# An RWKV-7 block: receptances read from their PSUM banks, key scaling on VectorE, the state summed in the bank, and the second inversion issued inside the recursion

## The chip, the cores and the metric

The kernel runs on one core of a Trainium2 chip. The metric is the device time of one execution in microseconds (us). The engines are named as in the profile: PE is TensorE's matmul, PEld its weight load, DVE is VectorE, ACT is ScalarE, POOL is GpSimd, SP is the queue that issues the DMAs. PSUM is the memory with eight banks that PE writes its products to; a bank holds 512 float32 values in each of 128 partitions.

## The reference

The program is a trunk of two layers on 512 positions of width 1024: SwiGLU, an attention mixer, SwiGLU; then SwiGLU, RWKV-7 time mixing, SwiGLU. Only the time mixing of the second layer changes:

```python
xr, xw, xk, xv, xa, xg = [h + xx * mix[i] for i in range(6)]   # xx: the row before, minus h
r, k, v = xr @ w_r, xk @ w_k, xv @ w_v
decay = exp(-exp(-softplus(-(w0 + tanh(xw @ w1) @ w2)) - 0.5))
a = sigmoid(a0 + (xa @ a1) @ a2)
kk = heads(k * k_k);  kk = kk / norm(kk)
k = k * (1.0 + (a - 1.0) * k_a)
# 16 heads of 64, one state S (64 x 64) a head, over the 512 positions:
S_t = S_{t-1} (diag(w_t) - kk_t^T (kk_t * a_t)) + v_t k_t^T;   y_t = S_t r_t
y = group_norm(y) + (sum(r * k * r_k) per head) * v
out = (y * g) @ w_o
```

r is called the receptance. The sequence is worked through in eight chunks of 64 positions: inside a chunk the recursion becomes a triangular system, whose inverse is applied, and only the state goes from chunk to chunk.

## The kernel before

Data lie features by positions: a tile of 128 features (two heads of 64) has 512 positions. There are two head groups, `sg` 0 and 1, of four such tiles (eight heads) each. A projection (`project(half, ...)`) makes four tiles at once, in four PSUM banks of the tag "rm" (there are four in all): for each of eight input blocks k it multiplies the mixed input with the weights into all four banks, in three passes of float32 split in two parts (L286 to L288 in `mm3`), 96 matmuls a half. The input blocks are mixed by `mixed(i, c)`: ACT scales (L1079), DVE adds the shifted row (L1081), ACT rounds to the high part (L1090), and DVE or POOL takes the residual (L1092). For the receptance (i = 0) the mixes are made anew for each half, in two alternating buffers.

The order in the program is: keys k half 0, prep of group 0, k half 1, v half 0 and 1, inversion of group 0, prep of group 1, receptance r half 0, `rw_prep2(0)`, r half 1, `rw_prep2(1)`, inversion of group 1, recursion of group 0, recursion of group 1. A scheduler then sets each engine's order from the dependencies, its own costs and the edges `self.after(a, b)`, which keep a behind b in the order without a wait on the chip. Each engine works through its own queue in that order.

`rw_prep` makes, for one tile, the decays, the normalised and scaled keys and the operands of the recursion: two matmul groups of "lora" products (`rq` banks), L1052 spreads the keys' norms, L1245 to L1261 are wide operations of 128 x 512 on DVE, L1248 is the key's product with its factor on POOL, L1268 multiplies operands chunk by chunk on PE, L1269 masks the result, and it goes to DRAM (L1282) to be laid out for the inversion. The scaled keys go to DRAM too (L1249).

`rw_inverse` loads that (`lin`), works off 31 pairs of DVE operations (L1321, L1325), reorders on ACT (L1326), writes the factors to DRAM (`tout`), reads them back, and finishes by a back-substitution in four blocks of 32 x 32 matmuls (L1353, L1360) with copies L1355 and L1362.

`rw_prep2` takes the receptances that ACT copied from the banks (L1102), multiplies them on POOL into the planes of the recursion (L1293), and on DVE with the reloaded keys (L1292, L1294) for the sum over each head on PE (L1297), copied by L1299.

`rw_recur(sg)` runs the chunks c = 0 to 7. A step solves for the chunk (L1422, L1427, ACT's L1433, L1437), copies the solution to `sv` (ACT L1440), forms the state's increment (L1445), multiplies the old state with its decay on POOL (L1448) and adds both on DVE (L1449; L1451 copies at c = 0). Then `rw_ties` prepares the next chunk (matmuls L1385, masks on DVE L1388, transposes L1391), and L1456 and L1461 make the outputs, which ACT copies (L1464).

Of the kernel before, what the change touches and what calls it, by code (L numbers as in the profile page):

```python
# [11 lines left out]
F32 = mybir.dt.float32  # L12
F32R = mybir.dt.float32r
AF = mybir.ActivationFunctionType
ALU = mybir.AluOpType
# [4 lines left out]
P = 128  # L20
D = 1024
S = 512
NCH = D // P
# [22 lines left out]
class Trunk:  # L46
# [1008 lines left out]
    def rwkv(self, gain):  # L1055
        nc, mm = self.nc, self.nc.tensor.matmul
# [8 lines left out]
        h = self.x  # L1065
# [6 lines left out]
        self.first = self.mid = None  # L1072
        n_mix = [0]

        def mixed(i, c):

            n = n_mix[0] = n_mix[0] + 1
            t = self.row("mx", 3) if i == 2 else self.rows[:, n % 2, :]
            ins = nc.scalar.activation(t, h[c], AF.Copy, scale=v["mix1"][:, i, c : c + 1])  # L1079
            self.after(ins, (self.mid, None, None, self.first)[i])  # L1080
            nc.vector.scalar_tensor_tensor(  # L1081
                out=t[:, 1:], in0=h[c][:, : S - 1], scalar=v["mix"][:, i, c : c + 1], in1=t[:, 1:],
                op0=ALU.mult, op1=ALU.add,
            )
# [5 lines left out]
            nc.scalar.copy(m[:, 0, :], t)  # L1090
# [4 lines left out]
        r_t, k_t = [None] * NCH, [None] * NCH  # L1095

        def evac_feature(dst):
            def f(half, ps):
                all4 = self.t("kr", [4, S], 2)
                for i in range(4):  # L1100
                    t = dst[4 * half + i] = all4[:, i, :]
                    nc.scalar.copy(t, ps[i])  # L1102
            return f

        vd = self.dram.tile([4, P, D], F32, name="vd")
        vcd = self.dram.tile([4, P, D], F32, name="vcd")
        kd = self.dram.tile([NCH, P, S], F32, name="kd")

        def evac_v(half, ps):

# [14 lines left out]

        def project(half, xm, evac, natural, i_mix=None):

            w, xs = [], xm if xm is not None else {}
            ps = [self.bank("rm", 4) for _ in range(4)]

            def tile(k, b):
                first, last = k == 0, k == NCH - 1
                if natural:
                    self.mm3(ps[b], tuple(t[:, b * P : (b + 1) * P] for t in xs[k]), w[k], first, last)
                else:
                    self.mm3(ps[b], tuple(t[:, b * P : (b + 1) * P] for t in w[k]), xs[k], first, last)

            for k in range(NCH):
                if k % 2 == 0:
                    w += self.next_w()  # L1140
                if half == 0 or xm is None:
                    if i_mix == 2:
                        normed(k)
                    xs[k] = mixed(i_mix, k)
                if k < 6:
                    for b in range(4):
                        tile(k, b)
                if k == 0 and half == 1 and not natural:
                    self.first = self.last_mm
# [9 lines left out]
        xm, evac = {}, evac_feature(k_t)  # L1159
        self.rwkv_hids()  # L1160
        project(0, xm, evac, False, 2)
        self.lora_hidden(lora_out, rstd)
        self.rr = {}
        self.rw = dict(r=r_t, k=k_t, vd=vd, vcd=vcd, kd=kd, w2a2=self.next_w())
        self.rw_norm(0)
        self.rw_prep_all(0)
        project(1, xm, evac, False)
        self.rw_norm(1)
        xm = {}
        project(0, xm, evac_v, True, 3)  # L1170
# [2 lines left out]
        self.rw_inverse(0, mid)  # L1173
        self.rw_prep_all(1)

        evac = evac_feature(r_t)
# [34 lines left out]
    def rw_prep(self, m):  # L1211

        nc, mm = self.nc, self.nc.tensor.matmul
# [31 lines left out]
        nc.vector.scalar_tensor_tensor(out=kk, in0=k, scalar=col("kk2"), in1=ps, op0=ALU.mult, op1=ALU.mult)  # L1245
        kx = cum
        nc.scalar.activation(kx, a, AF.Identity, scale=col("ka"), bias=col("ka1"))
        nc.gpsimd.tensor_tensor(out=k, in0=kx, in1=k, op=ALU.mult)  # L1248
        nc.sync.dma_start(rw["kd"][m], k)  # L1249
        nc.vector.scalar_tensor_tensor(out=a, in0=a, scalar=1.0, in1=kk, op0=ALU.add, op1=ALU.mult)  # L1250
        nc.vector.scalar_tensor_tensor(
            out=ar[:, 0, :, 1:], in0=ar[:, 0, :, 1:], scalar=-2.0, in1=ar[:, 1, :, : C - 1], op0=ALU.mult, op1=ALU.mult
# [29 lines left out]
                nc.sync.dma_start(dst, u[p0 : p0 + 32, :, 32 * s : 32 * s + 32])  # L1282
        yield

    def rw_prep2(self, sg):

        nc, rw = self.nc, self.rw
        ps = self.bank("rq", 3)[:8, :]
        for j in range(4):
# [3 lines left out]
            nc.gpsimd.tensor_tensor(out=rp, in0=r, in1=rp, op=ALU.mult)  # L1293
            nc.vector.scalar_tensor_tensor(  # L1294
                out=r, in0=r, scalar=self.v["rk"][:, m : m + 1], in1=k, op0=ALU.mult, op1=ALU.mult
            )
            nc.tensor.matmul(ps, self.sel[:, j, :], r, start=j == 0, stop=j == 3)  # L1297
        y = rw["r"][4 * sg][:8]
        nc.vector.tensor_copy(y, ps)  # L1299
        self.head_keep("b", sg, y)  # L1300

# [62 lines left out]
    def rw_ties(self, sg, c):  # L1364
# [20 lines left out]
                    prev, ins = ins, mm(ps[h][to, j, :], pp["kb"][e][own, c, :], pp["ar"][own, :, c, :], start=True, stop=True)  # L1385
                    self.after(ins, prev)
        for h in range(2):
            nc.vector.tensor_tensor(out=am[:, h], in0=ps[h], in1=mask, op=ALU.mult)  # L1388
# [14 lines left out]
    def rw_recur(self, sg):  # L1403

        nc, mm = self.nc, self.nc.tensor.matmul
        pairs = [self.rw[4 * sg + j] for j in range(4)]
# [9 lines left out]
        for c in range(NC):  # L1416
# [23 lines left out]
                nc.scalar.copy(sv[oth, h], ps[oth])  # L1440
            if c < NC - 1:
                ps = b2[:, 1]
                for j in range(4):
                    for h, (own, _) in enumerate(self.halves):
                        moved = mm(ps[own, j, :], bn[:, j, h, :], sv[:, h, j, :], start=True, stop=True)  # L1445
                if c:
                    pend = self.pend[:, sg, :, c, None].to_broadcast([P, 4, C])
                    nc.gpsimd.tensor_tensor(out=part, in0=st, in1=pend, op=ALU.mult)  # L1448
                    nc.vector.tensor_tensor(out=new, in0=ps, in1=part, op=ALU.add)  # L1449
# [158 lines left out]
```

## Time and profile before

| | us |
| --- | --- |
| median of three runs | 2159.97 |
| lowest, highest | 2156.48, 2165.26 |
| the profiled execution | 2156.56 |
| its span, first to last instruction | 2154.9 |

In the profiled execution PE is busy 2104.1 us, DVE 1165.4, ACT 781.2, POOL 192.7, and the mean granted clock of TensorE is 0.989. The part of the program that the change touches lies between about 1440 and 1735 us. A group of the profile is read: line, engine, operation, output and inputs by the program's names, shape, count, then the busy time with the mean of one in ns, then the idle time of the engine ahead of it and what ended that. A name like `const` or `inv` is that of the memory in which several tiles share a place: `const<-ra,const` at L1388 is the mask of the recursion.

### The profile page before, as it was taken

What the parts mean: (1) busy time and instruction counts of PE and PEld (TensorE: products, weight loads), DVE (VectorE), ACT (ScalarE), POOL (GpSimd) and SP (SyncE); (2) the same over time, 40 slices, a digit from 0 to 9 for tenths busy, and PEclk for the clock granted to TensorE, in tenths of its full rate; (3) what the DMA queues carried; (4) which work ended last, traced back from release to release, by engine and by line L of the source; (5) the groups of instructions that cost most, each with busy time, mean ns of one, the idle gap of its engine ahead of it and who ended that gap; (6) DMA issues with size and microseconds to landing.
All of it is one profiled execution on the core that took longest, in us unless ns stands there. A gap on an engine that the chain in (4) does not pass through costs nothing.

```text
span 2154.9 us, 28881 instructions
## 1 busy us (share of the span) xinstructions
PE 2104.1 (98%) x11623; PEld 1697.2 (79%) x11623; DVE 1165.4 (54%) x1595; ACT 781.2 (36%) x1180; POOL 192.7 (9%) x208
## 2 busy tenths in 40 slices
PE   8999999999999999999999999999978999999999
PEld 6888887767988888888888888777646768888887
DVE  5444444467568645446644454657675555444443
ACT  4222223355316433334433333472434434222222
POOL 2000001010002000002000000222451101000000
PEclk9999999999999999999999999999989999999999
DMA  5232323411117664555555555447743342232332
GB/s 180 78 110 86 109 87 108 125 57 47 28 45 231 217 200 158 183 187 180 181 182 162 183 160 189 170 137 234 220 131 85 102 131 86 83 113 93 98 103 59
DMA packets 264095, 286.59 MB, mean 133 GB/s; under 512 B 45140, under 2 KB 221420, under 8 KB 263961
## 3 DMA queue, kind: packets, MB, share of 16 engines
q1 hardware_dynamic: 261848, 282.65, 42.1%
q10 hardware_dynamic: 2112, 2.10, 0.3%
q8 instruction: 91, 1.49, 0.3%
q14 instruction: 44, 0.35, 0.1%
HBM read 229.85 MB, written 56.68 MB: 133 GB/s over the span
## 4 chain that ended last, share of the span: by engine, by line
PE 91%; DVE 6%; DMA 1%; issue 1%; ACT 1%; POOL 0%; SPq 0%; DVEq 0%; ACTq 0%; POOLq 0%
PE b L286 22%; PE b L288 22%; PE b L287 22%; PE am L286 3%; PE am L287 3%; PE am L288 3%; PE rm L286 1%; PE rm L287 1%; PE rm L288 1%; DVE const L1321 1%; PE wo L286 1%; PE rq L1021 1%; DVE inv L1325 1%; PE wo L287 1%; PE wo L288 1%
## 5 line engine op out<-in xcount | busy, mean ns | idle before, releaser
L287 PE MATMUL b<-xg,parts 128*128 128x512 f32 x1408 | 548.5, 390 | 0.0
L286 PE MATMUL b<-xg,parts 128*128 128x512 f32 x1408 | 547.0, 391 | 1.2 <-ACT xg L385 0.7
L288 PE MATMUL b<-xg,parts 128*128 128x512 f32 x1408 | 547.7, 390 | 0.0
L258 DVE TENSOR_TENSOR parts<-const,parts 128x1024 fp32r<-128x1024 f32 (+2 forms) x320 | 362.3, 1139 | 290.7 <-ACT parts L257 290.3
L257 ACT CAST parts<-const 128x1024 fp32r<-128x1024 f32 (+2 forms) x320 | 312.1, 977 | 469.2 <-PE b L287 391.0
L286 PEld LDWEIGHTS b<-xg,parts 128*128 128x128 f32 x1408 | 264.5, 188 | 57.2 <-ACT xg L385 1.1
L287 PEld LDWEIGHTS b<-xg,parts 128*128 128x128 f32 x1408 | 264.6, 188 | 56.6 <-issue 1.0
L288 PEld LDWEIGHTS b<-xg,parts 128*128 128x128 f32 x1408 | 264.4, 188 | 55.2 <-DVE parts L258 0.3
L288 PE MATMUL b<-act,parts 128*128 128x512 f32 x704 | 273.3, 389 | 0.0
L287 PE MATMUL b<-act,parts 128*128 128x512 f32 x704 | 273.2, 389 | 0.0
L286 PE MATMUL b<-act,parts 128*128 128x512 f32 x704 | 272.4, 390 | 0.0
L373 POOL TENSOR_TENSOR ssum<-ssum,sq 128x512 f32<-128x512 f32 x42 | 65.4, 1557 | 1201.2 <-ACT sq L372 534.4
L287 PEld LDWEIGHTS b<-act,parts 128*128 128x128 f32 x704 | 132.2, 188 | 27.5
L288 PEld LDWEIGHTS b<-act,parts 128*128 128x128 f32 x704 | 132.1, 188 | 27.3
L286 PEld LDWEIGHTS b<-act,parts 128*128 128x128 f32 x704 | 132.1, 188 | 27.2
L498 DVE SCALAR_TENSOR_TENSOR const<-b,const 128x512 f32<-128x512 f32 x128 | 87.3, 687 | 111.3 <-PE b L288 111.3
L291 ACT CAST act<-u 128x512 fp32r<-128x512 f32 x88 | 54.7, 622 | 245.4 <-DVE u L484 245.3
L483 DVE TENSOR_TENSOR u<-b,rstd 128x512 f32<-128x512 f32 x88 | 60.5, 690 | 146.6 <-PE b L288 146.4
L92 ACT ACTIVATE g<-g 128x512 f32<-128x512 f32 x88 | 55.1, 630 | 189.6 <-DVE g L478 189.6
L478 DVE TENSOR_TENSOR g<-b,rstd 128x512 f32<-128x512 f32 x88 | 60.3, 688 | 95.4 <-PE b L288 95.3
L292 DVE TENSOR_TENSOR act<-u,act 128x512 fp32r<-128x512 f32 x88 | 60.6, 689 | 36.8 <-ACT act L291 36.5
L484 DVE TENSOR_TENSOR u<-u,g 128x512 f32<-128x512 f32 x88 | 60.5, 691 | 2.7
(331 smaller groups left out, 2594.3 us busy)
## 6 DMA issues: line engine op xcount, KB each, us to landing
const<-in_ffn_w_gate_dram SPq DMA_DIRECT2D x88, 512.0 KB
const<-in_ffn_w_up_dram SPq DMA_DIRECT2D x88, 512.0 KB
parts<-pparts SPq DMA_DIRECT2D x68, 512.0 KB
parts<-parts SPq DMA_DIRECT2D x68, 512.0 KB
const<-in_ffn_w_down_dram SPq DMA_DIRECT2D x64, 512.0 KB
const<-in_ffn_w_down_dram SPq DMA_DIRECT2D x48, 256.0 KB
const<-in_attn_w_in_dram SPq DMA_DIRECT2D x24, 512.0 KB
lora<-pparts SPq DMA_DIRECT2D x8, 576.0 KB
```

What stands on the lines that cost most here:

```text
L92: ins = nc.scalar.activation(out, in_, func, **kw)
L257: self.nc.scalar.copy(hi[:r, :n], raw[:, :n])
L258: self.lo_engine.tensor_tensor(out=lo[:r, :n], in0=raw[:, :n], in1=hi[:r, :n].bitcast(F32), op=ALU.subtract)
L286: self.after(mm(out, lhs[0], rhs[0], start=start, stop=False), self.gate)
L287: mm(out, lhs[0], rhs[1], start=False, stop=False)
L288: self.last_mm = mm(out, lhs[1], rhs[0], start=False, stop=stop)
L292: self.nc.vector.tensor_tensor(out=lo, in0=t, in1=hi.bitcast(F32), op=ALU.subtract)
L373: nc.gpsimd.tensor_tensor(out=ssum, in0=ssum, in1=sq, op=ALU.add)
L478: nc.vector.tensor_tensor(out=g, in0=ps[i], in1=rstd, op=ALU.mult)
L483: nc.vector.tensor_tensor(out=u, in0=ps[2 + i], in1=rstd, op=ALU.mult)
L484: nc.vector.tensor_tensor(out=u, in0=u, in1=gs[i], op=ALU.mult)
L498: nc.vector.scalar_tensor_tensor(out=self.x[c], in0=ps, scalar=0.5, in1=self.x[c], op0=ALU.mult, op1=ALU.add)
```

## The change

The receptance's four banks are no longer copied by ACT. `rw_prep2` is called at the end of each receptance half and reads the banks with two DVE operations each: the product into the plane (L1282 of the changed kernel) and the product with the keys (L1283). The scaled keys stay in SBUF under a tag of their own; their way over DRAM is gone. The key's product with its factor is on DVE (L1239). The receptance's mixes have three buffers, and all mixes of a half hang on one point in the order. `dep` is the fifth input block's last matmul of the projection before (`self.mid`), and `r` in `rw_prep2` is the bank itself. In the recursion eight matmuls with an identity put the decayed state into the bank ahead of the increment's eight, and ACT copies the sum. The second inversion is issued in the first step of group 0's recursion.

```diff
@@ mixed(), project()
-            self.after(ins, (self.mid, None, None, self.first)[i])
+            self.after(ins, dep)
...
-            if i == 0:
-                m = self.shaped(self.parts_all[:, (n % 2) * 2 * S : (n % 2 + 1) * 2 * S], [2, S])
+            if i == 0 and n % 3:
+                m = self.shaped(self.parts_all[:, (n % 3 - 1) * 2 * S : n % 3 * 2 * S], [2, S])
             else:
-                m = self.pair("xm", 9, F32R)
+                m = self.pair("xm" if i else "xr", 9, F32R)
@@ rwkv()
-        project(0, None, evac, False, 0)
-        self.rw_prep2(0)
-        project(1, None, evac, False, 0)
-        self.rw_prep2(1)
-        self.rw_inverse(1, None)
-        self.rw_recur(0)
+        for half in range(2):
+            project(half, None, self.rw_prep2, False, 0)
+        self.rw_recur(0, lambda: self.rw_inverse(1, self.masked))
@@ rw_prep()
-        nc.gpsimd.tensor_tensor(out=k, in0=kx, in1=k, op=ALU.mult)
-        nc.sync.dma_start(rw["kd"][m], k)
+        nc.vector.tensor_tensor(out=k, in0=kx, in1=k, op=ALU.mult)
@@ rw_prep2(sg, rs)
-            k, r, rp = self.row("kback"), rw["r"][m], self.plane(sg, j, 1)
-            self.after(nc.sync.dma_start(k, rw["kd"][m]), self.mid)
-            nc.gpsimd.tensor_tensor(out=rp, in0=r, in1=rp, op=ALU.mult)
+            t, rp = self.row("rb"), self.plane(sg, j, 1)
+            nc.vector.tensor_tensor(out=rp, in0=r, in1=rp, op=ALU.mult)
             nc.vector.scalar_tensor_tensor(
-                out=r, in0=r, scalar=self.v["rk"][:, m : m + 1], in1=k, op0=ALU.mult, op1=ALU.mult
+                out=t, in0=r, scalar=self.v["rk"][:, m : m + 1], in1=rw["k"][m], op0=ALU.mult, op1=ALU.mult
             )
@@ rw_recur(sg, among=None)
                 if c:
                     nc.gpsimd.tensor_tensor(out=part, in0=st, in1=pend, op=ALU.mult)
-                    nc.vector.tensor_tensor(out=new, in0=ps, in1=part, op=ALU.add)
-                else:
-                    nc.vector.tensor_copy(new, ps)
+                    for j in range(4):
+                        for h, (own, _) in enumerate(self.halves):
+                            ins = mm(ps[own, j, :], self.ident[own, own], part[own, j, :], start=j == 0, stop=False)
...
+                nc.scalar.copy(new, ps)
                 am2, bn2, sv2 = self.rw_ties(sg, c + 1)
+                if c == 0 and among:
+                    among()
```

How this stands in the queues is seen at three places. The first is DVE's order at the end of prep of group 1. Before (`ra` is a bank of the ties, `rm` a bank of the receptance, `kr` its copy):

```order
L1269 TENSOR_TENSOR heads<-rq,const 128x512
L1388 TENSOR_TENSOR const<-ra,const 128x512 x2
L1269 TENSOR_TENSOR heads<-rq,const 128x512
L1294 SCALAR_TENSOR_TENSOR kr<-kr,const,kback 128x512 x2
L1269 TENSOR_TENSOR heads<-rq,const 128x512
L1294 SCALAR_TENSOR_TENSOR kr<-kr,const,kback 128x512 x2
L1299 COPY kr<-rq 8x512
L1321 TENSOR_TENSOR const<-const 128x31
```

The same place on DVE in the changed kernel:

```order
L1251 TENSOR_TENSOR heads<-const,heads 128x512
L1259 TENSOR_TENSOR heads<-rq,const 128x512 x3
L1283 SCALAR_TENSOR_TENSOR rb<-rm,const,k 128x512 x2
L1288 COPY rb<-rq 8x512
L292 TENSOR_TENSOR hids<-rb,hids 8x512
L1081 SCALAR_TENSOR_TENSOR const<-const 128x511 x3
L1282 TENSOR_TENSOR heads<-rm,heads 128x512
L1283 SCALAR_TENSOR_TENSOR rb<-rm,const,k 128x512
L1282 TENSOR_TENSOR heads<-rm,heads 128x512
```

Before, the four L1294 here belong to receptance half 1 and the second inversion follows; now the two L1283 are those of half 0's last two banks, and half 1's mixes and products follow.

The second place is PE's order in the same stretch. Before:

```order
L1052 MATMUL rq<-hids 128x512 x6
L286 MATMUL rm<-parts 128x512 x4
L287 MATMUL rm<-parts 128x512
L288 MATMUL rm<-parts 128x512
L287 MATMUL rm<-parts 128x512
L288 MATMUL rm<-parts 128x512
L287 MATMUL rm<-parts 128x512
L288 MATMUL rm<-parts 128x512
L287 MATMUL rm<-parts 128x512
L288 MATMUL rm<-parts 128x512
L1268 MATMUL rq<-heads 64x64 x16
```

And in the changed kernel (L1258 is what L1268 was, L1286 what L1297 was):

```order
L1052 MATMUL rq<-hids 128x512 x8
L1258 MATMUL rq<-heads 64x64 x64
L1286 MATMUL rq<-rb,const 8x512 x3
L286 MATMUL rm<-parts 128x512
L287 MATMUL rm<-parts 128x512
L288 MATMUL rm<-parts 128x512
```

The last of half 1's matmuls stood ahead of the first L1268; now 78 of the 96 stand behind all of L1258.

The third place is a step of group 0's recursion on PE. Before:

```order
L1427 MATMUL rr<-recur,heads 64x64 x8
L1385 MATMUL ra<-heads 64x128 x16
L1391 MATMUL ra<-const 128x128 x2
L1437 MATMUL rr<-recur,heads 64x64 x8
L1422 MATMUL rr<-const 64x64 x8
L1391 MATMUL ra<-const 128x128 x2
L1445 MATMUL rr<-const 64x64 x8
L1456 MATMUL rr<-const 64x64 x8
```

And in the changed kernel, where L1437 is now the identity matmul, L1426 what L1437 was, and L1443 what L1445 was:

```order
L1416 MATMUL rr<-recur,heads 64x64 x8
L1380 MATMUL ra<-const 128x128 x4
L1374 MATMUL ra<-heads 64x128
L1426 MATMUL rr<-recur,heads 64x64 x8
L1411 MATMUL rr<-const 64x64 x8
L1374 MATMUL ra<-heads 64x128 x15
L1437 MATMUL rr<-recur,const 64x64 x8
L1443 MATMUL rr<-const 64x64 x8
L1452 MATMUL rr<-const 64x64 x8
```

Eight matmuls more stand between the ties and the increment of the state.

More of the change, by code (lines that the diff above doesn't have):

```diff
@@ L1070, in normed, with mixed @@
             )
-        self.first = self.mid = None
+        self.mid = None
         n_mix = [0]
-        def mixed(i, c):
+        def mixed(i, c, dep=None):
             n = n_mix[0] = n_mix[0] + 1
@@ L1093, in mixed, with evac_k @@
             return m[:, 0, :], m[:, 1, :]
[L1095 to L1103, printed above, removed]
+        k_t = [None] * NCH
+        def evac_k(half, ps):
+            all4 = self.t("k", [4, S], 2)
+            for i in range(4):
+                t = k_t[4 * half + i] = all4[:, i, :]
+                nc.scalar.copy(t, ps[i])
         vd = self.dram.tile([4, P, D], F32, name="vd")
         vcd = self.dram.tile([4, P, D], F32, name="vcd")
-        kd = self.dram.tile([NCH, P, S], F32, name="kd")
         def evac_v(half, ps):
@@ L1126, in project @@
         def project(half, xm, evac, natural, i_mix=None):
-            w, xs = [], xm if xm is not None else {}
+            w, xs, dep = [], xm if xm is not None else {}, self.mid
             ps = [self.bank("rm", 4) for _ in range(4)]
@@ L1147, in project @@
                         tile(k, b)
-                if k == 0 and half == 1 and not natural:
-                    self.first = self.last_mm
                 if k == 4:
@@ L1401, in rw_ties, with rw_recur @@
         return am, bn, sv
-    def rw_recur(self, sg):
+    def rw_recur(self, sg, among=None):
         nc, mm = self.nc, self.nc.tensor.matmul
```

31 lines of the change are left out of this document (17 added, 14 removed).

## The prediction

> **What bounds the kernel now.** I read the page first: busy shares, then the chain that ended last.
>
> ```profile
> PE 2104.1 (98%) x11623; PEld 1697.2 (79%) x11623; DVE 1165.4 (54%) x1595; ACT 781.2 (36%) x1180; POOL 192.7 (9%) x208
> PE 91%; DVE 6%; DMA 1%; issue 1%; ACT 1%; POOL 0%; SPq 0%; DVEq 0%; ACTq 0%; POOLq 0%
> ```
>
> TensorE (PE) carries 91% of the chain, and a change that removes no matmul can win only what PE idles or runs at half clock. So I cut the stretch of the changed code into stages (busy time and instruction count of PE, PEld, DVE, ACT and POOL, then the granted clock, DMA share, GB/s):
>
> ```profile
> 1452.00:1477.00 25.00, 23.91 (x204) 16.66 (x203) 17.58 (x26) 6.33 (x10) 8.54 (x7) 1.00 0.55 166
> 1507.70:1538.60 30.90, 26.03 (x97) 19.66 (x95) 19.92 (x40) 12.29 (x18) 13.99 (x12) 0.89 0.88 265
> 1538.60:1572.35 33.75, 33.75 (x403) 23.57 (x402) 21.20 (x24) 22.43 (x37) 18.15 (x16) 1.00 0.56 158
> 1572.35:1598.30 25.95, 20.98 (x251) 14.41 (x250) 25.11 (x33) 6.63 (x15) 18.47 (x14) 0.87 0.62 176
> 1598.30:1619.42 21.12, 13.93 (x213) 9.13 (x212) 14.59 (x35) 5.19 (x13) 4.82 (x6) 0.84 0.23 59
> 1619.42:1663.30 43.88, 37.04 (x973) 30.95 (x974) 26.80 (x59) 18.11 (x43) 8.91 (x10) 0.92 0.34 87
> 1663.30:1732.50 69.20, 64.81 (x1082) 47.27 (x1073) 31.59 (x51) 29.29 (x71) 9.86 (x11) 0.98 0.37 110
> 1522.00:1525.41 3.41, 2.96 (x7) 2.38 (x8) 2.19 (x6) 1.41 (x2) 1.30 (x1) 0.50 0.08 32
> 1610.75:1617.58 6.83, 4.07 (x72) 3.62 (x74) 6.19 (x15) 2.72 (x7) 0.68 (x1) 0.50 0.00 1
> ```
>
> In order: prep of head group 0 beside the v projection; receptance half 0; half 1 with the back-substitution and the lora matmuls; prep of group 1 (there DVE is busy 25.11 of 25.95 us: it is the bound); the join to the recursion; group 0's recursion with the second inversion; group 1's recursion; two examples of half clock. The waits of PE in these stages (us, times, longest):
>
> ```profile
> PE rr L1422 <- DVE const L1388: 8.4, 4, 7.2
> PE rm L286 <- ACT parts L1090: 4.6, 2, 2.8
> PE rq L1268 <- DVE heads L1269: 3.6, 1, 3.6
> PE rr L1427 <- DVE recur L1449: 2.9, 4, 2.1
> PE rq L1353 <- DMA const<-tout: 2.1, 1, 2.1
> ```
>
> And the moments from which I build, on DVE and PE (start, duration, what was waited for):
>
> ```profile
> 1467.73 2.62 DVE L1269 TENSOR_TENSOR heads<-rq,const 128x512 f32<-128x512 f32 x4
> 1485.77 0.19 DVE L1321 TENSOR_TENSOR const<-inv 128x31 f32<-128x31 f32 x1 [0.99 <-DMA inv<-lin]
> 1524.17 0.19 DVE L1325 TENSOR_TENSOR inv<-inv,const 128x31 f32<-128x31 f32 x1
> 1527.13 1.41 DVE L1081 SCALAR_TENSOR_TENSOR const<-const 128x511 f32<-128x511 f32 x2 [2.76 <-ACT const L1079]
> 1538.63 0.24 PE L1353 MATMUL rq<-const,heads 32*32 32x32 f32 x2
> 1573.12 0.75 DVE L1245 SCALAR_TENSOR_TENSOR heads<-kr,const,rq 128x512 f32<-128x512 f32 x1 [4.27 <-PE rq L1052]
> 1574.62 1.64 DVE L1251 SCALAR_TENSOR_TENSOR heads<-heads 128x504 f32<-128x504 f32 x1
> 1587.86 0.67 DVE L1251 SCALAR_TENSOR_TENSOR heads<-heads 128x504 f32<-128x504 f32 x1
> 1597.69 0.68 DVE L1269 TENSOR_TENSOR heads<-rq,const 128x512 f32<-128x512 f32 x1
> 1605.85 0.19 DVE L1321 TENSOR_TENSOR const<-const 128x31 f32<-128x31 f32 x1 [3.69 <-DMA const<-lin]
> 1613.51 0.36 PE L1422 MATMUL rr<-const 64*64 64x64 f32 x1 [7.19 <-DVE const L1388]
> 1640.49 0.18 DVE L1325 TENSOR_TENSOR const<-const 128x31 f32<-128x31 f32 x1
> 1647.72 0.22 PE L1353 MATMUL rq<-const,heads 32*32 32x32 f32 x2 [2.11 <-DMA const<-tout]
> 1662.80 0.51 PE L1437 MATMUL rr<-recur,heads 64*64 64x64 f32 x10
> ```
>
> The first inversion runs on DVE from 1485.77 to 1524.36, the second from 1605.85 to 1640.67; group 0's last step is solved at 1662.8. The second inversion's end, plus 7.05 us until its factors are back from DRAM (1640.67 to 1647.72), sets when the back-substitution and with it that last step can go. So I ask of each part what it does to these moments. The costs by group (busy, mean ns | idle before them, releaser):
>
> ```profile
> L1248 POOL TENSOR_TENSOR kr<-heads,kr 128x512 f32<-128x512 f32 x8 | 13.2, 1676 | 3.3 <-DMA parts<-parts 2.0 <-DVE heads L1245 1.3
> L1293 POOL TENSOR_TENSOR heads<-kr,heads 128x512 f32<-128x512 f32 x8 | 12.2, 1555 | 0.0
> L1294 DVE SCALAR_TENSOR_TENSOR kr<-kr,const,kback 128x512 f32<-128x512 f32 x8 | 9.3, 1179 | 1.7 <-DMA kback<-kd 1.7
> L1260 DVE TENSOR_TENSOR heads<-kr,heads 128x512 f32<-128x512 f32 x8 | 5.6, 701 | 0.0
> L1102 ACT COPY kr<-rm 128x512 f32<-128x512 f32 x12 | 6.5, 593 | 0.7 <-PE rm L288 0.7
> L1449 DVE TENSOR_TENSOR recur<-rr,recur 128x256 f32<-128x256 f32 x12 | 5.0, 419 | 4.8 <-PE rr L1445 4.8
> L1464 ACT COPY heads<-rr 128x256 f32<-128x256 f32 x16 | 5.9, 371 | 16.8 <-PE rr L1461 14.1 <-PE rr L1456 2.6
> L1461 PE MATMUL rr<-heads,recur 64*64 64x64 f32 x224 | 10.0, 231 | 0.0
> 1458.62 0.39 PE L286 MATMUL rm<-parts,xm 128*128 128x512 f32 x1
> 1460.66 0.39 PE L286 MATMUL rm<-parts,xm 128*128 128x512 f32 x1
> ```
>
> **Part by part.** *Keys on DVE.* Four POOL products a group become four DVE ones of about 0.65 us (L1269: 2.62 for four; L1260, the same form, 0.70). On DVE that is +2.6 in prep of group 0, and the new order puts four more v mixes there (two took 1.41): +2.8. Against it, DVE no longer runs beside L1248: L1251 took 1.64 at 1574.62, where POOL multiplies, and 0.67 at 1587.86; with one such stretch of 1 us a product, the relief is 4 of the 5.4, and could be all. So PE, waiting at L1268 in the v projection, loses 0 to 7; I take +4. The inversion starts about 2.5 later, not 5, since 15.4 us lie between L1269's end (1470.35) and 1485.77, mostly DMA, with the four key writes of the group gone from SP's queue.
>
> *First inversion.* Three more receptance mixes (0.7 each) now stand inside it, and POOL's residuals come earlier: +4.5. End 1524.4 + 2.5 + 4.5 = 1531.4; bounds 1528 and 1534.
>
> *Receptance half 0.* In before three mixes follow the inversion, with 2.76 us for ACT's copy L1079 behind it; PE waits 4.6 and runs two windows of 3.41 us at half clock (3.4 lost). With all eight mixes ahead and three buffers I take 7 of these 8 as gone, bounds 0 and 8: end 1538.6 + 4 − 7 = 1535.6. Then the back-substitution needs the factors: 1531.4 + 2.1 (ACT's reorder) + 7.05 = 1540.5, 2 later than 1538.63.
>
> A page rule on the half clock: the Trainium skill, "TensorE: Matmul & The Clock Gate", Part 1, says that the clock falls after an idle window of about 3.4 us and returns after as long a busy one. By it gaps under 3.4 us would not be charged, and this term would be 4.6 instead of 7; the trace disagrees, with a clock of 0.50 around a wait of 2.8.
>
> *Banks held.* This is the largest move. L1294 becomes L1283, which reads the bank, and for banks 2 and 3 of half 0 it stands on DVE behind all of prep of group 1. PE's order fits that: half 1's first matmul into bank 2 stands behind the 64 of L1268, each sixteen of which wait for DVE, and what is queued behind them (78 of half 1's 96 matmuls, then the whole recursion) waits too. Only 18 run early. Ahead of the first L1052 before, 78 ran; now 18: 60 × 0.227 us (nine pitches in the 2.04 between the last two rows) = 13.6. The first L1245 comes at 1573.1 − 13.6 + 2 = 1561.5. The chain on DVE is then 28 wide operations at 0.6 to 0.7 and four tiny ones, 17 to 20, and some 2 for L1268 on a slow PE: 19.5, against 25.2 before (1573.12 to 1598.37), where POOL ran 18.47 of 25.95 beside it. L1269 ends at 1581, both L1283 at 1582.3. PE has meanwhile idled some 18 us. Then 78 × 0.227 = 17.7, plus 3.4 of half clock after the idling (two windows like those shown): half 1 ends at 1603.4. The second inversion stands on DVE behind half 1's last L1283, and its load on SP behind weight loads whose buffers half 1 frees as it ends: 1603.4 and about 3.7 of load (the wait at 1605.85) make 1607. Before: 1605.85. The earlier prep and the later projection cancel.
>
> *Receptances from the bank.* Eight of the twelve L1102 copies in that row (0.59 each) leave ACT, busy 12.29 of 30.90 us there: nothing, and if ACT had been full, 2.4 a half. Eight products of L1293 come to DVE (0.65 each): two groups of 2.6, the first in DVE's idle time after 1535, the second during half 1's matmuls but for the last bank's 1.3. The reload of the keys and its 1.7 us of waiting go; they lay in the 25.2 us of prep, in the sum above.
>
> *Recursion.* Step 0 no longer hides under prep; step 1 was behind the wait of 7.19 and the half clock around it (6.83 us, 3.4 lost). The first solves near 1606, the second near 1612; before, step 2 began at 1619.4, and now at 1618 to 1619. The second inversion loses five adds L1449 (2.1) and some stretching from its 34.8, but the masks among it wait for steps that start late, 1 to 2: 33.3, end 1640.3, bounds 1637 and 1644. The way on to 1662.8 stays, less part of the adds' 2.9 of wait: 1660.5, so −2 (−6 to +3).
>
> *State in the bank.* Twelve rounds of eight identity matmuls; L1461's 14 rounds took 10.0 us, 0.7 each, and their pitch among other work is nearer 0.6. In group 0 they lie where PE idles 6.8 of 43.88 us, and take the place of the wait for L1449; each waits for POOL's product of the state before, which has a whole step's time to be ready, and only L1443 (L1445 before) is queued behind it. If that cover is gone, they cost 3.6 there too. In group 1 PE is busy 64.81 of 69.20, so six rounds cost 3.6, less 0.6 for ACT's copy (0.37) in place of DVE's add (0.42 and its wait): +3, bounds 0 and 4.2.
>
> **Sum.** −2 for group 0 and +3 for group 1: +1, on the profiled execution's 2156.56. Its median of runs is 3.4 higher, 2159.97; from that the forecast is 2161.
>
> **Rivals.** *Faster.* The steps, not the inversion, set group 0's pace. For it: five of the adds sit between inversion rows, and PE waits 8.4 behind masks. Then the gain of 7 on receptance half 0 also reaches the inversion's start (v's +4 does not happen: POOL's relief pays it), and steps without the adds save one us each over six. Price: −7 − 6 + 3 = −10 against the sum above, and −4 more where the lost 3.4 of half clock before the remaining 78 isn't paid: 2148. Against it: the first inversion's DMA and the factors' 7.05 stay.
>
> *Slower: banks held too long.* If prep of group 1 keeps its 25.2 us, L1283 comes 5.7 later and the 78 matmuls, the inversion and the last step with it; the last three mixes stand on DVE behind it, and feeding them through ACT and POOL (1.5 a product there) adds 3; with all twelve identity rounds exposed, +3.6 more. 2161 + 12 = 2173. It decides from the moment that the last L1259 ends after 1586. The Trainium skill, "Perfetto Trace Analysis", Matmuls, asks that groups rotate through banks so that draining one overlaps the next one's matmuls; this change drains two banks only after 28 other operations. The trace of before shows no such hold, so its cost is my estimate from the rows.
>
> *The bank sum hides wholly.* ACT's copy shortens each step by the wait of 2.9 in total and group 1 pays nothing: 2158, no change either.
>
> **Chances.** No change (within 0.5%, 10.8 us, which is about what a measurement tells from nothing here) as in the sum, with or without the hidden bank sum: 0.5. Faster rival and beyond 0.26, slower 0.24. The range takes in most of both rivals, 2144 to 2178; the likeliest case alone is 2151 to 2171.
>
> **What would show it.** Right: a PE gap of 15 to 20 us in prep of group 1, with no wait L286 behind L1090; rm matmuls for some 18 us after the last L1259; the first row of the second inversion near 1606 and its last near 1640. The time is below the forecast if the second inversion starts before 1600, and above it if L1259 ends after 1586, or if the masks among the inversion wait over 5 us in all; the sum in the bank is wrong if L1443 is released by POOL's product.

## The result, and the profile after

The changed kernel takes 2173.61 us (median of nine runs, 2168.24 to 2176.62), against 2159.22 before (2151.59 to 2165.26): a ratio of 1.0071, 95% interval 1.0055 to 1.0088. It is slower by about 15 us. The profiled execution of the changed kernel took 2176.62 us, 20 more than that of before, so its rows show some 5 us more than the medians do.

Busy shares and the chain that ended last, from the page of the changed kernel:

```profile
PE 2118.9 (97%) x11815; PEld 1711.3 (79%) x11815; DVE 1164.8 (54%) x1597; ACT 782.5 (36%) x1186; POOL 165.4 (8%) x192
PE 90%; DVE 6%; ACT 1%; DMA 1%; issue 1%; POOL 0%; SPq 0%; DVEq 0%; ACTq 0%; POOLq 0%
```

PE has 192 more records (twelve rounds of eight matmuls, two records each) and 14.8 us more busy time. Where that lies, stage by stage in the changed kernel (the columns are those of the prediction's table): the back-substitution in two rows, the lora products and prep of group 1 in two, the held 78 matmuls, group 1's recursion, and the whole stretch from the first key operation of prep of group 0 to the last output projection:

```profile
1541.11:1551.35 10.24, 9.52 (x94) 6.97 (x95) 5.78 (x10) 2.64 (x4) 2.46 (x2) 0.50 0.85 187
1551.35:1558.17 6.82, 6.14 (x195) 4.69 (x195) 2.65 (x4) 1.69 (x3) 0.00 (x0) 1.00 0.01 2
1558.17:1573.80 15.63, 14.03 (x63) 8.21 (x55) 10.02 (x14) 12.43 (x21) 2.95 (x5) 0.50 0.09 27
1573.80:1588.89 15.09, 7.98 (x129) 7.26 (x130) 14.22 (x28) 1.13 (x2) 0.00 (x0) 0.50 0.08 14
1591.41:1612.20 20.79, 20.79 (x89) 15.16 (x89) 6.50 (x8) 5.79 (x9) 9.28 (x7) 1.00 0.69 210
1681.20:1753.10 71.90, 66.17 (x1084) 49.46 (x1078) 29.65 (x42) 29.12 (x70) 8.19 (x10) 0.95 0.35 102
1450.60:1812.10 361.50, 323.26 (x3766) 241.77 (x3767) 220.03 (x372) 138.83 (x271) 80.58 (x74) 0.91 0.43 128
```

The whole stretch and group 1's recursion in before:

```profile
1450.50:1791.10 340.60, 307.61 (x3565) 227.10 (x3564) 215.63 (x367) 133.57 (x257) 97.67 (x85) 0.94 0.50 148
1667.00:1730.40 63.40, 60.71 (x998) 44.10 (x993) 30.79 (x49) 26.45 (x63) 8.81 (x10) 0.97 0.37 109
```

The stretch grew by 20.9 us (361.5 by 340.6), which is the whole difference of the two executions (20.1) and a little more. PE is busy 15.7 us more (323.26 by 307.61) and idle 5.2 more (361.5 − 323.26 by 340.6 − 307.61). The added matmuls take at most 9.7 of the 15.7 (their group stands under run 2), so some 6 us or more are left for matmuls that run slower: the granted clock is 0.91 by 0.94. The longest waits of PE in the changed kernel (us, times, longest):

```profile
PE rq L1258 <- DVE heads L1251: 7.9, 4, 2.9
PE rm L286 <- DMA parts<-parts: 4.7, 2, 3.5
PE ra L1374 <- DVE heads L1282: 3.5, 1, 3.5
PE ra L1374 <- DVE const L1377: 3.0, 1, 3.0
PE rr L1411 <- DVE const L1377: 2.8, 2, 2.4
```

The mixes (L1090) no longer stop PE in receptance half 0; a weight load does (3.5, at 1520.05), and behind that half the first ties, which wait until DVE has multiplied the banks. The moments on DVE and PE that answer to those of before:

```profile
1450.59 0.75 DVE L1236 SCALAR_TENSOR_TENSOR heads<-k,const,rq 128x512 f32<-128x512 f32 x1 [1.92 <-PE rq L1052]
1488.97 0.19 DVE L1310 TENSOR_TENSOR const<-inv 128x31 f32<-128x31 f32 x1 [2.76 <-DMA inv<-lin]
1534.77 0.19 DVE L1314 TENSOR_TENSOR inv<-inv,const 128x31 f32<-128x31 f32 x1
1541.83 0.70 PE L1374 MATMUL ra<-heads 64*64 64x128 f32 x8 [3.54 <-DVE heads L1282]
1570.85 0.75 DVE L1236 SCALAR_TENSOR_TENSOR heads<-k,const,rq 128x512 f32<-128x512 f32 x1 [3.06 <-PE rq L1052]
1588.74 0.69 DVE L1259 TENSOR_TENSOR heads<-rq,const 128x512 f32<-128x512 f32 x1 [0.87 <-PE rq L1258]
1618.80 0.70 DVE L1310 TENSOR_TENSOR const<-const 128x31 f32<-128x31 f32 x1 [1.59 <-DMA const<-lin]
1651.44 0.19 DVE L1314 TENSOR_TENSOR const<-const 128x31 f32<-128x31 f32 x1
1677.93 0.27 PE L1426 MATMUL rr<-recur,heads 64*64 64x64 f32 x2
```

Both profiles begin this stretch at the same moment (first key operation at 1450.5 and 1450.6). The first inversion ends 10.6 later than before (1534.96 by 1524.36), the second starts 13.0 later, ends 11.0 later, and group 0's last step is solved 15.1 later (1677.9 by 1662.8). Group 1's recursion is 8.5 longer (71.90 by 63.40).

### The profile page after: what moved, and what is told of

It is laid out like the page before. It is cut to its first block, busy times and chain, and to the rows that moved or that the text cites. A ratio compares the mean times of both kernels' runs of the same rounds, so it can differ in the third digit from the quotient of the medians.

```text
span 2174.9 us, 29206 instructions
## 1 busy us (share of the span) xinstructions
PE 2118.9 (97%) x11815; PEld 1711.3 (79%) x11815; DVE 1164.8 (54%) x1597; ACT 782.5 (36%) x1186; POOL 165.4 (8%) x192
## 4 chain that ended last, share of the span: by engine, by line
PE 90%; DVE 6%; ACT 1%; DMA 1%; issue 1%; POOL 0%; SPq 0%; DVEq 0%; ACTq 0%; POOLq 0%
PE b L286 22%; PE b L287 22%; PE b L288 22%; PE am L286 3%; PE am L287 3%; PE am L288 3%; DVE const L1310 1%; PE rm L286 1%; PE rm L287 1%; PE rm L288 1%; PE wo L286 1%; PE wo L287 1%; PE wo L288 1%; DVE inv L1314 1%; DVE const L1314 1%
## 5 line engine op out<-in xcount | busy, mean ns | idle before, releaser
L287 PE MATMUL b<-xg,parts 128*128 128x512 f32 x1408 | 549.0, 390 | 0.0
L286 PE MATMUL b<-xg,parts 128*128 128x512 f32 x1408 | 546.7, 391 | 1.2 <-ACT xg L385 0.8
L288 PE MATMUL b<-xg,parts 128*128 128x512 f32 x1408 | 547.8, 390 | 0.0
L286 PEld LDWEIGHTS b<-xg,parts 128*128 128x128 f32 x1408 | 264.8, 188 | 57.7 <-ACT xg L385 1.2
L287 PEld LDWEIGHTS b<-xg,parts 128*128 128x128 f32 x1408 | 264.9, 188 | 56.0 <-issue 1.0
L288 PEld LDWEIGHTS b<-xg,parts 128*128 128x128 f32 x1408 | 264.7, 188 | 55.4 <-DVE parts L258 0.3
L288 PE MATMUL b<-act,parts 128*128 128x512 f32 x704 | 273.3, 389 | 0.0
L287 PE MATMUL b<-act,parts 128*128 128x512 f32 x704 | 273.2, 389 | 0.0
L286 PE MATMUL b<-act,parts 128*128 128x512 f32 x704 | 272.4, 390 | 0.0
L288 PEld LDWEIGHTS b<-act,parts 128*128 128x128 f32 x704 | 132.2, 188 | 27.6
L286 PEld LDWEIGHTS b<-act,parts 128*128 128x128 f32 x704 | 132.2, 188 | 27.3
L287 PEld LDWEIGHTS b<-act,parts 128*128 128x128 f32 x704 | 132.2, 188 | 27.1
L292 DVE TENSOR_TENSOR act<-u,act 128x512 fp32r<-128x512 f32 x88 | 60.5, 689 | 36.8 <-ACT act L291 36.5
```

The lines of the kernel that those rows point to most:

```text
L286: self.after(mm(out, lhs[0], rhs[0], start=start, stop=False), self.gate)
L287: mm(out, lhs[0], rhs[1], start=False, stop=False)
L288: self.last_mm = mm(out, lhs[1], rhs[0], start=False, stop=stop)
L292: self.nc.vector.tensor_tensor(out=lo, in0=t, in1=hi.bitcast(F32), op=ALU.subtract)
```

## The experiments

Ratios are to the kernel before on the same chip. All kernels below start from the changed kernel, and each run undoes parts of it.

**1. The hold of the banks.** The row "rb" has two buffers, and the product for bank 2 needs the first of them back. A matmul L1286 frees it, and this matmul stands on PE behind all of prep of group 1. Here the product overwrites the keys:

```diff
-            t, rp = self.row("rb"), self.plane(sg, j, 1)
+            t, rp = rw["k"][m], self.plane(sg, j, 1)
...
-        y = self.row("rb")[:8]
+        y = rw["k"][4 * sg][:8]
```

> The changed kernel, but the product of receptance and keys is written over the keys instead of into one of two rows 'rb'. Theory H (hold): the profile of the changed kernel shows the products of banks 2 and 3 at 1589 us, behind all of prep of group 1, because the two rows are freed by matmuls that stand on PE behind that prep; half 1's 78 matmuls wait for the banks, and PE, left with small matmuls alone, falls to half clock for 41 us (1541 to 1551 and 1558 to 1589). With the rows gone the banks are free at about 1547, half 1 runs among the back-substitution as before, and the second inversion starts 10 to 16 us earlier: 2157 to 2164 by 2174 of the changed kernel. Theory D (DVE load): the sixteen products that came to DVE in all are what delays; then the banks' release moves little, and the time stays within 4 us of 2174. Theory S (state in the bank): the loss is in the recursions; also within 4 us of 2174.

Measured: 2174.88, ratio 1.0077 (1.0061 to 1.0092), no different from the changed kernel. Half 1 ran among the back-substitution, as wanted, its last matmul 35 us earlier against the first key operation (126.4 us after it, by 161.6). But the second inversion started at the same distance, 168.4 by 168.2. DVE and PE of this run:

```profile
1615.82 0.19 DVE L1310 TENSOR_TENSOR const<-const 128x31 f32<-128x31 f32 x1 [10.11 <-DMA const<-lin]
1620.37 1.12 PE L1426 MATMUL rr<-recur,heads 64*64 64x64 f32 x16 [9.64 <-ACT recur L1422]
```

DVE now waits 10.11 us for the inversion's input, and PE 9.64 us ahead of the second step of group 0. Prep of group 1 came 9 to 12 later than in before or the changed kernel, since half 1's matmuls were ahead of it again and the first inversion ended as late as in the changed kernel (83.7 us after the first key operation; 73.8 before). So the hold isn't the cause by itself; whether the DVE work or the bank sum is was left open.

**2. The state in the bank.** The increment and the old state are added on DVE again, alone and with run 1's edit:

```diff
-                            ins = mm(ps[own, j, :], self.ident[own, own], part[own, j, :], start=j == 0, stop=False)
...
-                nc.scalar.copy(new, ps)
+                if c:
+                    nc.vector.tensor_tensor(out=new, in0=ps, in1=part, op=ALU.add)
+                else:
+                    nc.scalar.copy(new, ps)
```

> The changed kernel, but old state and increment are added on DVE as before (no identity matmuls, no copy of the sum on ACT; step 0's copy stays on ACT). Theory S: twelve rounds of eight matmuls at 0.6 us cost 3.6 us in group 1's recursion and up to as much in group 0's; group 1's steps took 70.6 us from step 0 to step 7's start-to-start against 62.7 before, so 2167 to 2171. Theory H: group 0's part is hidden by the inversion, group 1's is worth 3 to 4: 2170. Rival: the longer group 1 is chance (a DMA wait of 2.2 us and a half-clock window of 6.8 us), then no change from 2174 beyond 2 us; or the add's waits between the inversion's rows come back in group 0 and it is slower, 2177.

> Both: keys overwritten in place, and the state added on DVE. Theory H with S: the gains add, 2153 to 2160, faster than before by 0 to 6 us. If the bank sum had helped group 0's recursion once the hold is gone, this is not faster than the kernel with the rows gone alone.

Measured: 2165.84, ratio 1.0031 (1.0019 to 1.0043), and 2165.51, 1.0032 (1.0018 to 1.0045). The bank sum costs 8.6 us (1.0071 − 1.0031, of 2159) without the edit of run 1 and 9.7 with it, about three times the +3 of the prediction's sum; the intervals of each pair lie apart. The identity's group in the changed kernel, and group 1's recursion in the run with the add on DVE:

```profile
L1437 PE MATMUL rr<-recur,const 64*64 64x64 f32 x192 | 9.7, 239 | 2.8 <-ACT const L1429 2.3 <-issue 0.4
1671.50:1738.80 67.30, 62.57 (x982) 46.08 (x978) 31.77 (x48) 27.21 (x64) 8.29 (x10) 0.95 0.38 110
```

A round is 9.7 / 12 = 0.81 us of PE. In group 1's recursion, at the same clock, PE is busy 66.17 with the bank sum and 62.57 without (3.6 for six rounds), and the stage is 4.6 longer. In group 0, from step 1 to step 7, it takes 54.8 us with and 51.6 without. Together 7.8.

**3. The second inversion's place.**

```diff
-        self.rw_recur(0, lambda: self.rw_inverse(1, self.masked))
+        self.rw_inverse(1, None)
+        self.rw_recur(0)
```

> The changed kernel, but the second inversion is issued ahead of group 0's recursion, as before. Theory H: its place changes little while half 1 ends at 1612 us: within 4 us of 2174. Rival: issuing it behind the first masks is itself what delays it; then it starts some us earlier, and group 0's steps fall in line behind it: 2166 to 2170, or, if the masks now queue behind it as they did for 7.2 us before, 2178 or more.

Measured: 2173.16, ratio 1.0066 (1.0048 to 1.0084): no change. It did start 22 us earlier (145.8 us after the first key operation), but it stretched to 43.7 us, since half 1 of the receptance now ran beside it and put three mixes and eight products of its banks among the rows (7.8 of the 10.8 us by which it is longer). Group 0's last step was solved at 230.7 by 227.3.

**4. Mixes and keys undone, one at a time.** The mixes: two buffers and the old edges (that part of the diff reversed). The keys:

```diff
-        nc.vector.tensor_tensor(out=k, in0=kx, in1=k, op=ALU.mult)
+        nc.gpsimd.tensor_tensor(out=k, in0=kx, in1=k, op=ALU.mult)
```

> The changed kernel, but the mixes as before: two buffers for the receptance's, and the old edges in the order. Theory I (first inversion): in the changed kernel the first inversion lies 3.1 us later than before at its start and 10.5 at its end (each against the first key operation of prep of group 0), 3.8 of it from four more mixes that stand among its rows, 2 from three small norm operations; this delay is carried to the end. With five mixes among its rows again it ends 4 to 7 earlier: 2167 to 2170, by 2174. Theory P (the late projection and the slow PE behind it): the mixes' buffers had taken PE's wait in receptance half 0 away, and giving them up costs up to 3: 2174 to 2177.

> The changed kernel, but the key's product with its factor on POOL again (the keys stay in SBUF). Theory I: prep of group 0 ends up to 2.4 earlier on DVE, and prep of group 1 takes 18.6 us plus the stretching beside POOL less four products: 2172 to 2176, no clear change, since what DVE saves by four products of 0.6 it loses beside POOL. If the products on DVE are themselves the loss, 2169 or less. If POOL's stretching is as costly as in before (25 us of prep against 18.6), 2178 or more.

Measured: 2183.10, ratio 1.0117 (1.0090 to 1.0144), and 2180.88, 1.0107 (1.0079 to 1.0134): each made the changed kernel slower, by 10 and 8 us. No theory of the first run had that. The second number lies in the last case of its expectation (2178 or more), but not for the reason given there: prep of group 1 took 19.3 us in that run, not 25. With the old mixes the first inversion did end earlier (75.5 us after the first key operation, by 84.4) and the second began 4.5 earlier; but in that run half clock was granted for 82 us of the stretch, against 65 in the changed kernel, and the lead was gone by group 0's last step. Undoing one part beside the hold doesn't give its price.

**5. Three parts undone, with the hold and without.**

> The changed kernel with three parts undone: mixes as before, key product on POOL, state added on DVE. What is left is the receptances read from their banks, the keys kept in SBUF and the place of the second inversion. Theory I: the state's 8 and the first inversion's 4 to 7 add up: 2158 to 2162, level with before. Theory P: the state's 8 alone: 2164 to 2168.

> Only the receptances read from their banks, with the keys overwritten in place, and the keys kept in SBUF without the way over DRAM; mixes, key product, state and the second inversion's place as before. Theory I: the parts that delay the first inversion and lengthen the steps are gone; eight copies on ACT, eight products on POOL and sixteen transfers are saved, twelve us of DVE time beside POOL come back: level with before or up to 6 faster, 2153 to 2160. Theory P: reading the banks on DVE is what delays group 1's prep or the recursion: 2164 or more.

> The kernel with the banks alone (receptances from the banks with the keys overwritten in place, keys kept in SBUF; mixes, key product, state as before), but the second inversion is issued inside the recursion, as in the changed kernel. Against the run with three parts undone (2175) it differs in the hold alone. Theory H2: the hold costs only where nothing ahead of it is late, and so costs here what the two earlier runs differ by: 2149 to 2156. Theory K: the place inside the recursion is what costs, since the load then follows the first masks and small copies queue behind DVE's wait for it; then 2165 or more, and the hold is worth little.

Measured: with the hold 2175.32, ratio 1.0088 (1.0062 to 1.0115); without it and with the inversion ahead 2149.21, 0.9959 (0.9945 to 0.9973); without it and with the inversion inside 2148.31, 0.9959 (0.9945 to 0.9974). The last two are the fastest kernels of this study, 9 us faster than before, and equal, so the place is worth nothing here either. The first and the third differ in two lines, those of run 1, which changed nothing there: here they are worth 28 us. The stretch and the stage of the lora products in the run with the hold, then the same without it (there the second row is the back-substitution and the lora products with half 1 among them):

```profile
1450.70:1808.20 357.50, 317.71 (x3566) 233.03 (x3565) 216.86 (x373) 130.68 (x251) 83.78 (x77) 0.91 0.44 129
1549.30:1583.40 34.10, 23.57 (x205) 15.94 (x199) 27.07 (x39) 13.75 (x22) 9.28 (x9) 0.50 0.09 19
```

```profile
1450.40:1785.20 334.80, 305.09 (x3569) 224.60 (x3568) 218.27 (x373) 131.08 (x251) 84.40 (x77) 0.96 0.46 138
1541.40:1570.00 28.60, 28.33 (x331) 19.90 (x330) 16.62 (x24) 19.46 (x32) 9.81 (x11) 1.00 0.45 139
1606.80 0.19 DVE L1312 TENSOR_TENSOR const<-const 128x31 f32<-128x31 f32 x1 [0.42 <-DMA const<-lin]
```

The two stretches differ by 22.7 us. With as many matmul records (3569 and 3566) PE is busy 305.09 us without the hold and 317.71 with it, at a clock of 0.96 and 0.91. So 12.6 of the 22.7 are the same matmuls running slower, and 10.1 are more idling of PE.

With the runs before, this makes a square. All four kernels add the state on DVE and have the second inversion inside; its start is again counted from the first key operation, and the profiled execution of the third lay 8.5 us above its median:

| | ratio to before (95%) | second inversion starts |
| --- | --- | --- |
| neither hold nor new mixes and keys | 0.9959 (0.9945 to 0.9974) | 156.4 |
| the hold alone | 1.0088 (1.0062 to 1.0115) | 167.0 |
| new mixes and keys on DVE alone (run 2 with run 1's edit) | 1.0032 (1.0018 to 1.0045) | 169.2 |
| both (run 2 alone) | 1.0031 (1.0019 to 1.0043) | 166.6 |

Mixes and keys together cost 16 us without the hold and gain 12 beside it, which agrees with run 4, where undoing either one made the kernel slower. Why they gain there is not settled.

**6. Up the ladder.** From the last kernel, parts are put back one at a time: the keys' product on DVE; then the new mixes; then the state in the bank (the second inversion ahead in all three, which costs nothing).

> The kernel with the banks alone, and the key's product on DVE. Prep of group 0 ends about 2 later and with it the first inversion; prep of group 1 loses POOL's stretching but gains four products. Theory I: 2149 to 2153, no clear change by 2149. Theory L: the sixteen stores of the inversion's input, which went out in two lots before and in one lot of 7.7 us in the run with the keys in place, come at once behind the denser DVE order: 2154 to 2160.

> The kernel with the banks alone, the key's product on DVE, and the new mixes (three buffers, new edges); state on DVE, second inversion ahead of the recursion. Theory I: eight mixes among the first inversion's rows delay its end by 7 to 10, and with half 1 no longer held this reaches the end: 2157 to 2163. Rival (the mixes' gain in receptance half 0 stays, as the run with the old mixes was 9 slower in the changed kernel): 2143 to 2149.

> The changed kernel with the keys overwritten in place and the second inversion ahead of the recursion: all that the last run has, and the state in the bank. Theory S: the state's identity matmuls cost the 8 us that they cost in the changed kernel: 8 above the last run. Rival: the 8 came from that kernel's late steps, and are 3 to 4 here (six rounds of 0.6 us in group 1).

| kernel | median us | ratio to before (95%) | step, us of 2159 |
| --- | --- | --- | --- |
| banks alone, inversion inside | 2148.31 | 0.9959 (0.9945 to 0.9974) | −9 |
| banks alone, inversion ahead | 2149.21 | 0.9959 (0.9945 to 0.9973) | 0 |
| + keys on DVE | 2155.72 | 0.9990 (0.9978 to 1.0001) | +7 |
| + new mixes | 2164.15 | 1.0036 (1.0021 to 1.0050) | +10 |
| + state in the bank | 2173.60 | 1.0069 (1.0048 to 1.0090) | +7 |
| + inversion inside (run 1) | 2174.88 | 1.0077 (1.0061 to 1.0092) | +2 |
| + hold (the changed kernel) | 2173.61 | 1.0071 (1.0055 to 1.0088) | −1 |

The steps 0, +2 and −1 lie within the intervals. The mixes' step is seen in the first inversion. DVE's mixes from its first row to its last (the last mix of each count begins as the inversion ends), the end of prep of group 1 (its last masks, L1262 and L1260), and the wait at the start of the second inversion, without the new mixes and with them:

```profile
L1081 DVE SCALAR_TENSOR_TENSOR const<-const 128x511 f32<-128x511 f32 x6 | 4.5, 745 | 0.0
1593.51 0.67 DVE L1262 TENSOR_TENSOR heads<-rq,const 128x512 f32<-128x512 f32 x1
1602.34 0.27 DVE L1313 TENSOR_TENSOR const<-const 128x31 f32<-128x31 f32 x1 [2.18 <-DMA const<-lin]
```

```profile
L1081 DVE SCALAR_TENSOR_TENSOR const<-const 128x511 f32<-128x511 f32 x9 | 7.8, 869 | 0.0
1601.60 1.87 DVE L1260 TENSOR_TENSOR heads<-rq,const 128x512 f32<-128x512 f32 x3
1614.45 0.19 DVE L1311 TENSOR_TENSOR const<-const 128x31 f32<-128x31 f32 x1 [9.66 <-DMA const<-lin]
1600.48 7.73 SPq L1273 DMA_DIRECT2D lin<-heads  x16
```

In the same distances the first inversion runs from 33.6 to 75.2 and from 38.4 to 84.2, later by 4.8 at its start and 9 at its end, and the second starts at 152.8 and 168.5. Of these 15.7 us, 9 are there as the first inversion ends, and 12.9 as the last mask of prep of group 1 ends (157.5 by 144.6). The other 2.8 arise behind that mask: with the new mixes all sixteen stores of the second inversion's input are issued in one lot of 7.73 us, ahead of its load, and without them the first four went out earlier.

The keys' step is not seen where it was looked for. With the product on DVE the second inversion starts and ends earlier (152.8 and 186.8 us, by 156.4 and 190.6 in the kernel with the inversion inside), and group 0's last step stands level (208.2 by 208.0). The difference lies in group 1: that stage in the kernel with the product on POOL, and on DVE, with PE's longest wait in the second of them:

```profile
1662.70:1724.60 61.90, 59.63 (x1000) 44.11 (x994) 30.56 (x48) 27.09 (x64) 9.24 (x10) 1.00 0.37 112
1661.30:1731.40 70.10, 64.71 (x1007) 47.30 (x1002) 33.14 (x50) 28.29 (x67) 8.97 (x11) 0.95 0.35 104
PE rr L1414 <- DMA bs<-vcd: 1.9, 2, 1.3
```

Of the 8.2 us, PE is busy 5.1 more, at most 3.5 of it by the clock ((1 − 0.95) × 70.1), and idle 3.1 more. The wait for the values' load (`bs<-vcd`, 1.9) does not occur in the kernel with the product on POOL, nor in before. What a product in prep has to do with that stage, other than a new order of everything behind it, is not settled.

## Why the prediction was right or wrong

The time lies in the range given, near its upper end, because the range took in both rivals and not because the sum held. The likeliest case, 2161 and no change, was wrong by 13 us, and the sign was the slower rival's.

**The rival had the number and not the mechanism.** "Banks held too long" gave 2173 and named the sign, a last L1259 after 1586; it ended at 1589.4. But prep of group 1 did not keep its 25.2 us. From 1570.85 to 1589.43 it took 18.6, as forecast (19.5). It began 9.3 late. So 2173 was met partly by luck. And releasing the banks alone gains nothing (run 1), because then the late first inversion holds up the second to the same moment. The square under run 5 shows it: the second inversion starts at 167.0 with the hold alone, at 169.2 with mixes and keys alone, at 166.6 with both, and at 156.4 with neither. They are two ways to one late moment, and don't add up. That start doesn't give the time by itself: with the inversion ahead (run 3) it came at 145.8 and nothing was won, and the hold alone is 12 us slower than both.

**The first inversion: mis-sized.** The forecast was an end of 1531.4 with an upper bound of 1534; it was 1534.96. The start was right (1488.3 by 1488.97). Its length is 46.0 us by 38.6. Three more mixes stand among its rows, as forecast (eight by five), but one of them was stretched to 1.85 beside POOL. Three small operations on the norms (L292, L404, L407, 0.7 each) moved in too, and were not in the sum.

**Receptance half 0: the gain turned into other waits.** 7 us were to go. The wait on L1090 went, but PE now waits 3.5 for a weight load and 3.5 for L1282, which stands on DVE behind the next mixes; the half's last matmul ends at 1538.3, where 1535.6 was forecast and 1539.8 was seen before.

**The clock: the step that failed.** I allowed 3.4 us for half clock, after PE's idling in prep of group 1. The clock was at 0.50 from 1541.1 to 1551.3 and from 1558.2 to 1588.9, 41 us, and both began before that idling. The first began at the end of PE's new wait of 3.54 us ahead of L1374 (1541.83), the second among small matmuls. The changed kernel up to the first L1236 and through prep of group 1:

```profile
1541.11:1570.85 29.74, 26.76 (x332) 18.16 (x332) 15.61 (x23) 13.84 (x24) 4.80 (x6) 0.61 0.31 68
1570.85:1589.43 18.58, 11.44 (x136) 9.07 (x137) 17.60 (x33) 4.05 (x5) 0.60 (x1) 0.51 0.12 29
```

Up to L1236 PE is busy for nine tenths of the time, and (1 − 0.61) × 29.74 = 11.6 us are lost to the clock at most; that is about the 9.3 by which L1236 came late (1570.85, forecast 1561.5). Behind it DVE is the bound, busy 17.60 of 18.58 us, so the half clock cost little there. I counted the 13.6 us by which 60 large matmuls less would bring prep of group 1 forward, and left out that these matmuls were what ran between the small ones at full clock; that the clock fell for want of them is argued in the last section. PE's gap in prep of group 1 was 7.1 us in all (18.58 − 11.44), not the 15 to 20 that were to be the sign.

**The second inversion: right in length, on a late start.** Its length was forecast as 33.3 us and was 32.8. The start was 1618.8 by 1607: 8.8 of the 11.8 are there as half 1 ends (1612.2 by 1603.4), 3 are a longer way from there to the first row (6.6 by 3.6). From its end to group 0's last step it is 26.3 us, where 20.2 was forecast and 22.1 seen before.

**The state in the bank: the term was +3, and measured +7 to +10** in three pairs. The round is 0.81 us and not 0.6, and the cover in group 0 isn't there (54.8 by 51.6). By the order on PE the round stands between the solution and L1443, so it lengthens the chain through the step for which PE waits; that this is the reason is argued, not tried. The sign that was to show this term wrong, L1443 released by POOL's product, did not appear (its three waits end on ACT), and the term was wrong all the same.

**Keys on DVE: +4 in the v projection, and nothing behind it.** In the ladder the product costs 7, and its rows show that in group 1's recursion, for which I had no term.

**The faster rival's number by another way.** Its 2148 is the time of the kernel with the banks alone, but it was to come from the new mixes and from steps without the adds, and that kernel has neither. Reading the banks directly, with the keys kept in SBUF, is worth 9 us when the products that free them don't wait on something that stands behind the next stage. Without the two-buffer row and the three other parts, this change makes the kernel faster.

## What to carry to other kernels

A bank that is read by its consumer instead of being copied out is held by everything that the consumer needs: here a second buffer of a scratch row, freed by a matmul in another queue, in a bank handed out in program order. Write the product over an operand that is done, or give it buffers enough, and look in the order where each release stands. When several parts delay the same moment, undoing one can show nothing, or even a loss (run 4); undo all and put them back one at a time. A step of the ladder is then a part's price on top of those below it, not its price in every kernel.

## What the runs showed of the hardware

Half clock lasted for 30.72 us though PE was busy for 14.03 of the first 15.63 of them. What it ran there, in the changed kernel (groups of that window; L287 and L288 have the form of L286):

```profile
L286 PE MATMUL rq<-hids,parts 64*128 64x512 f32 x7 | 4.4, 744 | 1.3 <-DVE heads L1351 0.8 <-ACT heads L92 0.5
L1052 PE MATMUL rq<-hids 8*128 8x512 f32 x8 | 4.1, 665 | 0.3 <-ACT pa L92 0.2
L1349 PE MATMUL rq<-heads,inv 32*32 32x32 f32 x34 | 1.0, 223 | 0.0
```

These multiply over 64, 8 and 32 rows. Before, the same matmuls ran with 79 of 128 x 512 among them (1538.60 to 1572.35, busy throughout), and the clock was 1.00. The Trainium skill ("TensorE: Matmul & The Clock Gate", Part 1) has the full clock come back after some 3.4 us of sustained activity. PE busy for nine tenths of 15.63 us, more than four such windows, did not bring it back here. That the matmuls' small size is why fits the six profiles of this study with the hold, each with half clock for 30.7 or 34.1 us at that place, and no kernel without the hold has such a stretch there; but no run tried the size by itself.
